# A state-space scan's small products in three bunches a group instead of four, with the last output weights moved ahead of the last norm

## The chip, the core and the metric

One core of a Trainium2 chip runs the whole model in one launch. The metric is device time in microseconds (us): the median of the timed runs. Engines are named as in the profile: PE (matrix products), DVE, ACT and POOL (elementwise work), SP (issues the transfers).

## The reference

One sequence of 512 tokens, width 1024, float32, goes through two layers; each is a mixer and then a channel mixer, both added to the input. The channel mixer (`conv_ffn`) is an up projection to 44 tiles of 128 channels, a causal convolution of three taps, gate times up, and a down projection. Layer 0 mixes by dilated attention. Layer 1 mixes by a scan, and the change is mostly there. Cut to what matters, in chunks of 128 tokens:

```
zxbcdt = h @ w_in                              # z, x, B, C, dt
x, B, C = silu(conv4(x, B, C)); dt = softplus(dt + bias)
a_cs   = cumsum(dt * a) in a chunk;  xdt = x * dt
cb     = C @ B^T                               # one 128x128 block a chunk and group
y_diag = (cb * exp(a_cs_i - a_cs_j), j <= i) @ xdt
states = B^T @ (xdt * exp(a_cs_last - a_cs));  prev = scan of states over the chunks
y      = y_diag + (C @ prev) * exp(a_cs) + d_skip * x
g      = y * silu(z);  y = g * rsqrt(mean(g*g over the group's 256 channels) + eps) * norm_w
out    = x_in + y @ w_out
```

There are 8 groups (B, C and the norm are per group) with 4 heads of 64 channels each, so a group has two x tiles and two z tiles of 128 channels. A last norm follows layer 1.

## The kernel before

Activations lie with 128 channels on the partitions and all 512 tokens along the free dimension. Every projection is done in three float32r products: weights and activations are split into a high and a low part (`hi`/`lo`, `xh`/`xl`, made by ACT and DVE, for z tiles by POOL), and `mm3` multiplies high by high, high by low and low by high. One output tile of 128 channels is thus 24 matmuls of 128x128 by 512 ("a projection"), all of line L127. A weight tile of 512 KB (`raw_...`) is loaded by SP, three in flight, and five pairs `hi`/`lo` exist. Products of projections land in three `mm` banks of PSUM; the small products use three `aux` and two `side` banks.

In layer 1, `project_group(g, ...)` lists six projections of a group: x0, b, c, x1, z0, z1. `scan_group(g, ...)` is a generator that does the rest of a group. Its products, by the names of their outputs:

- px (xs transposed, for each half x = 0 and 1; DVE makes xdt of it and POOL xdd), pb (B transposed, copied to btok), pc (C times B; DVE masks it into cb);
- pst (states, from xdd and btok); a chain of one copy, two multiplications and two additions on DVE turns it into prev;
- py (from lm and xdt) and pf (from C and prev); lm is a row of a_cs copied from HBM to 128 partitions by SP, then four subtractions on DVE, an Exp on ACT and a product with cb on POOL; ee is the Exp of the same rows;
- ss (column sums of gsq, the squares of the gated output yt; DVE makes ms, POOL the power rg) and prg (rg laid along the free dimension), after which yt is scaled and split into `y{g}{x}` high and low.

Output weights are applied group-wise: `w01` (groups 0 and 1), `w23`, `w4`, `w56`, and `w7` in `last_group`, each eight steps (one per 128 output channels); DVE adds each product to the residual xr. A step for one group is 6 matmuls, for two groups 12.

The order on PE within layer 1 is written by hand (`manual_schedule`): `groups` weaves the pieces of `behind(g)`, which are the generator's steps of group g and the norm of group g-1, with a list `fill` of projections of group g+1 and output steps. A group has four bunches of small products with `(17, 24, 21, 38)` as shares of the filling. `last_group` treats group 7, the output steps left over, and the first products of the next channel mixer (`u1_0` to `u1_3`) between the last norm's parts. On DVE, ACT, POOL and mostly SP a scheduler in the compiler orders the work by its own estimates; only a part marked otherwise is fixed.

At the start eight products of ones by ones (`warm`) run while the first weights arrive, and products called v follow. The final channel mixer multiplies gate and up (`au`) and takes its low part (`g21l` for the last pair) on POOL, at L543 and L546.

Of the kernel before, what the change touches and what calls it, by code (L numbers as in the profile page):

```python
# [51 lines left out]
def trunk(ctx: ExitStack, tc: tile.TileContext, A, out):  # L52
# [20 lines left out]
    def side_bank(name):  # L73
        return ps.tile([P, 512], F32, tag="side", name=name, bufs=2)
# [196 lines left out]
    xps = []  # L271
    load, first = v_steps(1, 0, 2)
    warm = side_bank("warm")
    for _ in range(8):
        T.matmul(warm[:, 0:P], ones, ones, start=True, stop=True)
    with tc.manual_schedule(engines={mybir.EngineType.SP}):
        for k in range(KD):
# [250 lines left out]
    def ffn(layer, done):  # L528
        for part, (c0, cn) in enumerate(FF_PARTS):
            gh, gl = [], []  # L530
            for c in range(c0, c0 + cn):
                ab = []
                for gu in range(2):
                    i = 2 * c + gu
                    n = f"u{layer}_{i}"
                    p = project(A["wup"][layer * 44 + i], n)
                    us = t2("us" + n, "us", 3, lp)
                    V.tensor_tensor(us, p, rbc, op=ALU.mult)  # L538
                    a = t2("a" + n, "a", 13, lp)
                    conv(a, us, C_FCW + (layer * 44 + i) * 3, C_FCB + layer * 44 + i, 3)  # L540
                    ab.append(a)
                SC.activation(ab[0], ab[0], AF.Silu)
                G.tensor_tensor(ab[1], ab[0], ab[1], op=ALU.mult)  # L543
                g_h, g_l = high_low(f"g{c}")
                SC.copy(g_h, ab[1])
                G.tensor_tensor(g_l, ab[1], g_h.bitcast(F32), op=ALU.subtract)  # L546
                gh.append(g_h)
                gl.append(g_l)
            n = cn * P

            def load(m):
                i = (layer * len(FF_PARTS) + part) * KD + m
                return (*load_unit(A["wdn"][i][:, :n], f"wd{i}", n), 0)

            def add(m, p):
                V.tensor_tensor(xr[m], xr[m], p, op=ALU.add)  # L556
                if part == len(FF_PARTS) - 1:
                    done(m)
# [106 lines left out]
    def scan_group(g, d, ys):  # L665
# [17 lines left out]
        def states(x):  # L683
            pst = aux_bank("pst")
            for c in range(3):
                cs = slice(c * P, (c + 1) * P)
                T.matmul(pst[:, cs], btok[:, cs], xdd[x][:, cs], start=True, stop=True)
            t = t2("prev", "prev", 1, lp)
            SC.copy(t[:, 0:P], pst[:, 0:P])
            for c in range(1, 3):  # L690
                now, was = slice(c * P, (c + 1) * P), slice((c - 1) * P, c * P)
                V.tensor_tensor(
                    two(t[:, now]), two(t[:, was]),
                    cd3[:, c, heads[x]].unsqueeze(2).to_broadcast([P, 2, 64]), op=ALU.mult,
                )
                V.tensor_tensor(t[:, now], t[:, now], pst[:, now], op=ALU.add)
            prev.append(t)
# [17 lines left out]
                lm.append(t)  # L715
            ee.append(e_)

        def outputs(x):
            py, pf = side_bank("py"), side_bank("pf")


            with tc.manual_schedule(engines={mybir.EngineType.PE}):
                for c in range(NCH):
                    cs = slice(c * P, (c + 1) * P)
                    for hp in (1, 0):
                        T.matmul(
                            py[hp * 64 : (hp + 1) * 64, cs],
                            xdt[x][:, c * P + hp * 64 : c * P + (hp + 1) * 64], lm[2 * x + hp][:, cs],
                            start=True, stop=True,
                        )  # L730
                for c in reversed(range(1, NCH)):
                    T.matmul(  # L732
                        pf[:, c * P : (c + 1) * P], prev[x][:, (c - 1) * P : c * P],
                        ct[:, c * P : (c + 1) * P], start=True, stop=True,
                    )
            yt = t2("yt", "yt", 2, lp)
            V.tensor_tensor(ee[x][:, P:512], ee[x][:, P:512], pf[:, P:512], op=ALU.mult)
            V.scalar_tensor_tensor(
                yt, xs[x], col(C_DSK + 2 * g + x), py, op0=ALU.mult, op1=ALU.add
            )  # L740
            V.tensor_tensor(yt[:, P:512], yt[:, P:512], ee[x][:, P:512], op=ALU.add)
            V.tensor_tensor(yt, yt, d[f"z{x}"], op=ALU.mult)
            sq = t2("gsq", "sq", 2)
            SC.activation(sq, yt, AF.Square)
            return yt, sq
# [5 lines left out]
            T.transpose(pb[:, c * P : (c + 1) * P], bt[:, c * P : (c + 1) * P], ident)  # L751
        btok = t2("btok", "btok", 1, lp)
        SC.copy(btok[:, 0:384], pb[:, 0:384])
        pc = aux_bank("pc")
        for c in range(NCH):
            cs = slice(c * P, (c + 1) * P)
            T.matmul(pc[:, cs], bt[:, cs], ct[:, cs], start=True, stop=True)
# [3 lines left out]
            tri.unsqueeze(1).to_broadcast([P, NCH, P]), op=ALU.mult,  # L761
        )
        yield
        decays(0)
        states(0)
        by_token(1)
        yield
        y0, sq0 = outputs(0)
        decays(1)
        states(1)  # L770
        yield
        y1, sq1 = outputs(1)
        V.tensor_tensor(sq0, sq0, sq1, op=ALU.add)
        yield
        rg = sm.tile([P, 4], F32, tag="rg", name="rg")
# [44 lines left out]
    writes = [[], [], w01[:4], w01[4:], w23[:4], w23[4:], w4[:4]]  # L820
    scans = []

    def behind(g):

        scans.append(scan_group(g, tiles[g], ys))
        for i in range(4):
            next(scans[g])
            if g and i < 2:
                next(scans[g - 1], None)
            yield  # L830

    def groups():
        decays = decay_rates()
        next(decays)
        for i, f in enumerate(ahead[0] + ahead[1][:1]):
            f()
            if i == 1:
                next(decays)
        next(decays, None)
        for g in range(NSG - 1):  # L840
            a, w = ahead[g + 1], writes[g]
            if g == 0:
                fill = a[1:]
            elif g == NSG - 2:
                fill = [a[0], a[1], w[0], w[1], a[2], w[2], w[3], a[3]]
            else:
                fill = a[:3]
                n = -(-len(w) // 3)
                for i, f in enumerate(a[3:]):
                    fill = fill + w[i * n : (i + 1) * n] + [f]  # L850
            weave(behind(g), (17, 24, 21, 38) if g else (1, 1, 1, 2), fill)

    def last_group():

        z0, z1 = ahead[NSG - 1][4:]
        core = behind(NSG - 1)  # L860
        for fill in ([z0, w4[4]], [z1, w4[5]], [w4[6], w4[7], w56[0]], w56[1:5]):
            next(core)
            for f in fill:
                f()
        scan = scans[-1]
        load7, w7 = write_groups([7], ys)
        next(scan)
        w56[5]()
        load7(0)
        units = []  # L870

        def unit(i):
            name = f"u1_{i}"
            units.append((
                load_unit(A["wup"][44 + i], name), side_bank(name) if i in (1, 2) else mm_bank(name), name
            ))

        def part(i, *ks):
            if i == len(units):
                unit(i)  # L880
            (hi, lo), t, _ = units[i]
            for k in ks:
                mm3(t, hi, lo, k, xh[k], xl[k], k == 0, k == KD - 1)

        with tc.manual_schedule(engines={mybir.EngineType.DVE, mybir.EngineType.Activation}):
            next(scan, None)
            w56[6]()
            w56[7]()
            unit(0)
            load7(1)  # L890
        for m in range(5):
            w7[m]()
        part(0, 0)
        w7[5]()
        part(0, 1)
        part(1, 0)
        w7[6]()
        part(0, 2)
        part(1, 1)
        part(2, 0)  # L900
# [12 lines left out]
        part(3, *range(4, KD))  # L913
        for _, t, name in units:
            early[name] = t

    with tc.manual_schedule(engines={mybir.EngineType.PE}):
        groups()
        last_group()


    def finish(load, operand, cn):
# [135 lines left out]
```

## Time and profile before

| what | value |
|---|---|
| median of 3 runs | 1686.44 us (1686.26 to 1686.98) |
| the profiled execution, its own time | 1686.95 us |
| its span, first to last instruction | 1685.2 us |
| PE, DVE, ACT, POOL busy | 98%, 63%, 41%, 27% |
| mean granted clock of PE | 0.995 |
| scan layer, first x0 projection to first product of u1 | 871 to 1310 us: 439.0 us, PE busy 421.85 |

In the profile a row of a timeline gives the start and the length in us, then engine, line, operation, output and inputs; brackets give the engine's idle time before it and what ended that. A row of groups ends with total busy time and mean ns of one, then the idle time before. A float32 product of small tiles leaves two records, a float32r one or a transpose one. PEclk is the granted share of PE's clock, 1.00 or 0.50 here.

### The profile page before, as it was taken

Reading aid. Unit: us, or ns where it says so; the run is one execution under the profiler, and the core shown is the slowest. Engines: PE = TensorE matmul, PEld = TensorE weight load, DVE = VectorE, ACT = ScalarE, POOL = GpSimd, SP = SyncE. Lnnn points to the kernel's source line nnn. Section 1 sums busy time; section 2 is a strip of 40 time slices with the busy share of each in tenths; the row PEclk is TensorE's granted clock in tenths of the full one; section 3 lists DMA queues with packets and bytes.
Section 4 is the critical chain, followed back from the end, with each engine's and each line's share of the span. In section 5 each row is a group of like instructions: output and inputs, shape, how many; then the busy total and the mean of one; then the engine's idle time right before and its main releaser. Section 6 shows DMA issues by size and latency. Waiting matters only on the chain.

```text
span 1685.2 us, 21510 instructions
## 1 busy us (share of the span) xinstructions
PE 1656.1 (98%) x8224; PEld 1403.1 (83%) x8224; DVE 1066.3 (63%) x1794; ACT 698.8 (41%) x1022; POOL 462.8 (27%) x305
## 2 busy tenths in 40 slices
PE   9999999999999999999999899999989999999997
PEld 8888888888888888888888777888878788888887
DVE  5366564366657745745657788777786784574564
ACT  5233332333245423423346665455552542342345
POOL 0443443144413211211242222332230341121124
PEclk9999999999999999999999999999999999999999
DMA  6322222222223223223233232333221332322323
GB/s 225 112 77 74 88 76 88 92 84 75 81 95 125 100 88 113 100 87 102 75 115 119 88 100 94 105 102 100 101 82 42 121 104 86 111 100 88 113 76 125
DMA packets 52342, 165.56 MB, mean 98 GB/s; under 512 B 5840, under 2 KB 8144, under 8 KB 52240
## 3 DMA queue, kind: packets, MB, share of 16 engines
q1 hardware_dynamic: 51152, 163.15, 28.7%
q8 instruction: 65, 1.06, 0.3%
q10 hardware_dynamic: 1088, 1.05, 0.2%
q14 instruction: 37, 0.30, 0.1%
HBM read 162.01 MB, written 2.16 MB: 97 GB/s over the span
## 4 chain that ended last, share of the span: by engine, by line
PE 91%; DVE 5%; issue 1%; ACT 1%; POOL 1%; DMA 1%; POOLq 0%; SPq 0%; DVEq 0%; ACTq 0%
PE u L127 28%; PE qk L127 15%; PE wd L127 12%; PE v L127 8%; PE z L127 5%; PE xs L127 5%; PE wso L127 4%; PE b L127 2%; PE wz L127 2%; PE wo L127 1%; PE c L127 1%; PE pp L410 1%; PE pg L423 1%; PE po L418 1%; PE pf L732 1%
## 5 line engine op out<-in xcount | busy, mean ns | idle before, releaser
L127 PE MATMUL u<-xl,hi_u 128*128 128x512 f32 x704 | 270.3, 384 | 0.8 <-DVE xl L176 0.8
L127 PE MATMUL u<-xh,hi_u 128*128 128x512 f32 x704 | 270.4, 384 | 0.0
L127 PE MATMUL u<-xh,lo_u 128*128 128x512 f32 x704 | 270.0, 384 | 0.0
L543 POOL TENSOR_TENSOR au<-au,au 128x512 f32<-128x512 f32 x44 | 57.9, 1316 | 434.9 <-DVE au L523 414.3
L118 ACT CAST hi_u<-raw_u 128x1024 fp32r<-128x1024 f32 x88 | 91.2, 1044 | 196.9 <-PE u L127 101.9
L523 DVE SCALAR_TENSOR_TENSOR au<-usu,par,au 128x510 f32<-128x510 f32 (+1 forms) x176 | 160.9, 919 | 5.9 <-ACT au L521 1.0
L325 POOL TENSOR_TENSOR rotqk<-rotqk,sr 32x512 f32<-32x512 f32 x48 | 91.8, 1913 | 257.6 <-DVE rotqk L324 214.4
L127 PEld LDWEIGHTS u<-xl,hi_u 128*128 128x128 f32 x704 | 131.9, 187 | 26.8 <-DVE xl L176 1.8
L127 PEld LDWEIGHTS u<-xh,lo_u 128*128 128x128 f32 x704 | 131.9, 187 | 25.3
L127 PEld LDWEIGHTS u<-xh,hi_u 128*128 128x128 f32 x704 | 131.9, 187 | 25.3
L127 PE MATMUL qk<-xh,hi_qk 128*128 128x512 f32 x384 | 149.1, 388 | 0.0
L127 PE MATMUL qk<-xl,hi_qk 128*128 128x512 f32 x384 | 148.2, 386 | 0.0
L127 PE MATMUL qk<-xh,lo_qk 128*128 128x512 f32 x384 | 147.1, 383 | 0.0
L538 DVE TENSOR_TENSOR usu<-u,rbc 128x512 f32<-128x512 f32 x88 | 60.5, 690 | 112.7 <-PE u L127 103.3
L119 DVE TENSOR_TENSOR lo_u<-raw_u,hi_u 128x1024 fp32r<-128x1024 f32 x88 | 112.9, 1289 | 22.1 <-ACT hi_u L118 22.1
L556 DVE TENSOR_TENSOR xr<-xr,wd 128x512 f32<-128x512 f32 x40 | 27.2, 687 | 116.7 <-PE wd L127 116.7
L118 ACT CAST hi_qk<-raw_qk 128x1024 fp32r<-128x1024 f32 x48 | 50.1, 1045 | 102.5 <-PE v L127 52.5
L321 DVE TENSOR_TENSOR qk<-qk,cr 128x512 f32<-128x512 f32 x48 | 33.0, 688 | 91.0 <-PE qk L127 90.7
L118 ACT CAST hi_wd<-raw_wd 128x1024 fp32r<-128x1024 f32 (+1 forms) x56 | 52.4, 951 | 76.7 <-PE wd L127 39.7
L127 PEld LDWEIGHTS qk<-xh,lo_qk 128*128 128x128 f32 x384 | 72.0, 188 | 13.2
L127 PEld LDWEIGHTS qk<-xh,hi_qk 128*128 128x128 f32 x384 | 72.0, 188 | 12.8
L127 PEld LDWEIGHTS qk<-xl,hi_qk 128*128 128x128 f32 x384 | 72.1, 188 | 12.3
(635 smaller groups left out, 3969.4 us busy)
## 6 DMA issues: line engine op xcount, KB each, us to landing
raw_u<-in_wup SPq DMA_DIRECT2D x88, 512.0 KB, 3.2
raw_qk<-in_wqk SPq DMA_DIRECT2D x48, 512.0 KB, 3.2
raw_wd<-in_wdn SPq DMA_DIRECT2D x32, 512.0 KB, 3.2
raw_wd<-in_wdn SPq DMA_DIRECT2D x24, 384.0 KB, 3.1
raw_xs<-in_win SPq DMA_DIRECT2D x16, 512.0 KB, 3.2
raw_z<-in_win SPq DMA_DIRECT2D x16, 512.0 KB, 3.3
lm<-rows SPq DMA_DIRECT2D x32, 256.0 KB, 4.1
raw_wso<-in_wso SPq DMA_DIRECT2D x16, 512.0 KB, 3.2
```

Of the source, the lines that this page charges most:

```text
L118: SC.copy(hi[:, s], raw[:, s])
L119: low.tensor_tensor(lo[:, s], raw[:, s], hi.bitcast(F32)[:, s], op=ALU.subtract)
L127: T.matmul(in_turns(dst), w, in_turns(x), start=first, stop=last)
L321: V.tensor_tensor(at(t), of(p), of(cr), op=ALU.mult)
L325: G.tensor_tensor(rot[R, :], rot[R, :], sr[R, :], op=ALU.mult)
L410: T.transpose(pp[:, b * P : (b + 1) * P], pr[:, b * P : (b + 1) * P], ident)
L418: T.matmul(po[:, ii], v0[h][:, b * P : (b + 1) * P], pts[i][:, (b - i + 1) * P : (b - i + 2) * P], start=b == max(i - 1, 0), stop=b == i,)
L423: T.matmul(pg[:, ii], vt[g, half][i][:, es], pts[i][:, (g + 1) * P : (g + 2) * P], start=g == 1, stop=g == 2,)
L523: V.scalar_tensor_tensor(dst[:, j:], src[:, : S - j], col(c_w + taps - 1 - j), dst[:, j:], op0=ALU.mult, op1=ALU.add,)
L538: V.tensor_tensor(us, p, rbc, op=ALU.mult)
L543: G.tensor_tensor(ab[1], ab[0], ab[1], op=ALU.mult)
L556: V.tensor_tensor(xr[m], xr[m], p, op=ALU.add)
```

## The change

1. `scan_group` is cut into three bunches a group: A is px of half 0, pb, px of half 1 and pc (and ss of the group before); B is both pst (and prg of the group before); C is both py and then both pf. The two halves have their own prev (two buffers instead of one), and py and pf of half 1 use aux banks, pc a side bank.
2. `between(g)` writes out what stands between two bunches: two projections, with output steps added to them. For the last group all eight steps of `w4` stand between A and B, z1 and two steps of `w56` between B and C, and two more of `w56` behind C.
3. `last_rows` puts one step of `w56` between ss and prg of the last group and three behind prg, and loads both units of `w7` and the first of u1 ahead of that.
4. The decay rates' last products (pa, prow) stand ahead of x0 of group 1 instead of behind it.
5. Eleven instead of eight `warm` products. The last pair of the last channel mixer is multiplied and split on DVE instead of POOL.

```diff
-    for _ in range(8):
+    for _ in range(11):
         T.matmul(warm[:, 0:P], ones, ones, start=True, stop=True)
...
-                G.tensor_tensor(ab[1], ab[0], ab[1], op=ALU.mult)
+                by = V if layer == 1 and c == NFF - 1 else G
+                by.tensor_tensor(ab[1], ab[0], ab[1], op=ALU.mult)
...
-                G.tensor_tensor(g_l, ab[1], g_h.bitcast(F32), op=ALU.subtract)
+                by.tensor_tensor(g_l, ab[1], g_h.bitcast(F32), op=ALU.subtract)
...
-            t = t2("prev", "prev", 1, lp)
+            t = t2("prev", "prev", 2, lp)
...
-        def outputs(x):
-            py, pf = side_bank("py"), side_bank("pf")
+        def products(x):
+            py, pf = (side_bank("py"), side_bank("pf")) if x == 0 else (aux_bank("py"), aux_bank("pf"))
...
+            def carried():
                 for c in reversed(range(1, NCH)):
                     T.matmul(
                         pf[:, c * P : (c + 1) * P], prev[x][:, (c - 1) * P : c * P],
                         ct[:, c * P : (c + 1) * P], start=True, stop=True,
                     )
+                return py, pf
+            return carried
+        def outputs(x, py, pf):
...
         SC.copy(btok[:, 0:384], pb[:, 0:384])
-        pc = aux_bank("pc")
+        by_token(1)
+        pc = side_bank("pc")
...
         yield
-        decays(0)
-        states(0)
-        by_token(1)
+        for x in range(2):
+            states(x)
+        for x in range(2):
+            decays(x)
         yield
-        y0, sq0 = outputs(0)
-        decays(1)
-        states(1)
-        yield
-        y1, sq1 = outputs(1)
+        carried = [products(x) for x in range(2)]
+        (y0, sq0), (y1, sq1) = (outputs(x, *banks) for x, banks in enumerate([f() for f in carried]))
         V.tensor_tensor(sq0, sq0, sq1, op=ALU.add)
...
-        for i in range(4):
+        for i in range(3):
             next(scans[g])
...
+    def between(g):
+        if g < NSG - 1:
+            x0, b, c, x1, z0, z1 = ahead[g + 1]
+        if g < NSG - 3:
+            after = ahead[g + 2][0]
+            return [
+                [[b, c], [x1, z0], [z1, after]],
+                [[b, c], [x1, z0], [z1, after]],
+                [[b, c], [x1, z0], [z1, *w01[:2], after]],
+                [[b, w01[2], c], [x1, w01[3], z0], [z1, *w01[4:6], after]],
+                [[b, w01[6], c], [x1, w01[7], z0], [z1, *w23[:2], after]],
+            ][g]
+        if g == NSG - 3:
+            return [b, w23[2], c], [x1, w23[3], z0], [z1, *w23[4:6]]
+        if g == NSG - 2:
+            return [x0, b], [c, x1], [z0, *w23[6:]]
+        return w4, [ahead[g][5], *w56[:2]], w56[2:4]
...
-        for i, f in enumerate(ahead[0] + ahead[1][:1]):
+        for i, f in enumerate(ahead[0]):
...
         next(decays, None)
-        for g in range(NSG - 1):
...
-            weave(behind(g), (17, 24, 21, 38) if g else (1, 1, 1, 2), fill)
+        ahead[1][0]()
+        for g in range(NSG):
+            for _, fill in zip(behind(g), between(g)):
+                for f in fill:
+                    f()
...
         next(scan)
-        w56[5]()
+        w56[4]()
         load7(0)
+        load7(1)
...
+        unit(0)
         with tc.manual_schedule(engines={mybir.EngineType.DVE, mybir.EngineType.Activation}):
             next(scan, None)
-            w56[6]()
-            w56[7]()
-            unit(0)
-            load7(1)
+            for m in range(5, KD):
+                w56[m]()
```

The order on PE, small products of group 1 (and the norm of group 0), the rows of L127 between them left out. Before:

```order
L674 MATMUL px<-ident,axs_7085 128x128 x4
L751 MATMUL pb<-ident,ab_7161 128x128 x3
L757 MATMUL pc<-ac_7238,ab_7161 128x128 x4
L196 MATMUL ss<-ones,gsq 128x1 x4
...
L687 MATMUL pst<-xdd,btok 128x128 x3
L674 MATMUL px<-ident,axs_7329 128x128 x4
L208 MATMUL prg<-ident,rg 128x128 x4
...
L726 MATMUL py<-lm,xdt 64x128 x8
L732 MATMUL pf<-ac_7238,prev 128x128 x3
L687 MATMUL pst<-xdd,btok 128x128 x3
```

A fourth bunch, py and pf of half 1, follows. Now, on the same engine and for the same group:

```order
L676 MATMUL px<-ident,axs_7103 128x128 x4
L760 MATMUL pb<-ident,ab_7173 128x128 x3
L676 MATMUL px<-ident,axs_7309 128x128 x4
L767 MATMUL pc<-ac_7212,ab_7173 128x128 x4
L196 MATMUL ss<-ones,gsq 128x1 x4
...
L689 MATMUL pst<-xdd,btok 128x128 x6
L208 MATMUL prg<-ident,rg 128x128 x4
...
L728 MATMUL py<-lm,xdt 64x128 x16
L736 MATMUL pf<-ac_7212,prev 128x128 x6
```

Both px now stand in the first bunch, both pst in the second, and both halves' py and pf in the third.

The order on POOL from a low part of z of group 2 (lo_z) through group 1's work to the power rg that prg of group 0 needs. Before:

```order
L119 TENSOR_TENSOR lo_z_7745<-raw_z_7743,hi_z_7744 128x1024
L677 TENSOR_TENSOR xdd<-xdt,dec 128x384
L714 TENSOR_TENSOR lm<-lm,cb 128x512 x4
L202 TENSOR_TENSOR rg<-ms,mhalf 128x4
L119 TENSOR_TENSOR lo_z_7779<-raw_z_7777,hi_z_7778 128x1024
```

Now:

```order
L119 TENSOR_TENSOR lo_z_7695<-raw_z_7693,hi_z_7694 128x1024
L119 TENSOR_TENSOR lo_z_7770<-raw_z_7768,hi_z_7769 128x1024
L679 TENSOR_TENSOR xdd<-xdt,dec 128x384 x2
L716 TENSOR_TENSOR lm<-lm,cb 128x512 x4
L202 TENSOR_TENSOR rg<-ms,mhalf 128x4
```

Ahead of rg there now stand a second lo_z and a second xdd.

The order on ACT at the last group, from the Exp of its rows (ee) to the first cast of the weights for w56 (hi_wso). Before:

```order
L706 ACTIVATE ee<-lm 64x384 x2
L647 ACT_TABLE_LOAD
L647 ACTIVATE ab_9775<-ab_9775 128x512
L744 ACTIVATE gsq<-yt 128x512
L713 ACT_TABLE_LOAD
L713 ACTIVATE lm<-lm 128x512 x2
L118 CAST hi_z_10106<-raw_z_10105 128x1024
L521 ACTIVATE ac_9888<-usc_9886,par 128x512
L118 CAST hi_wso_10216<-raw_wso_10215 128x1024
```

Now:

```order
L708 ACTIVATE ee<-lm 64x384 x4
L649 ACT_TABLE_LOAD
L649 ACTIVATE axs_9821<-axs_9821 128x512
L118 CAST hi_z_10120<-raw_z_10119 128x1024
L753 ACTIVATE gsq<-yt 128x512 x2
L715 ACT_TABLE_LOAD
L715 ACTIVATE lm<-lm 128x512 x3
L645 ACT_TABLE_LOAD
L645 ACTIVATE usz_9899<-usz_9899 128x512
L715 ACT_TABLE_LOAD
L715 ACTIVATE lm<-lm 128x512
L118 CAST hi_wso_10154<-raw_wso_10153 128x1024
```

The cast now stands behind all four ee and all four lm of the last group.

The order on DVE at the same place, from xdt of the last group to the first addition of a w4 product. Now:

```order
L678 TENSOR_TENSOR xdt<-px,dtt 128x512
L119 TENSOR_TENSOR lo_wso_10155<-raw_wso_10153,hi_wso_10154 128x1024
L678 TENSOR_TENSOR xdt<-px,dtt 128x512
L119 TENSOR_TENSOR lo_wso_10161<-raw_wso_10159,hi_wso_10160 128x1024
L769 TENSOR_TENSOR cb<-pc,tri 128x512
L201 TENSOR_SCALAR ms<-ss 128x4
L812 TENSOR_TENSOR xr_4036<-xr_4036,wso_9976 128x512
```

Before, the first four w4 products were added ahead of that xdt; now the first addition stands behind two low parts.

More of the change, by code (lines that the diff above doesn't have):

```diff
@@ L716, in decays @@
             ee.append(e_)
-        def outputs(x):
-            py, pf = side_bank("py"), side_bank("pf")
[L722 to L730, printed above, removed]
+        def products(x):
+            py, pf = (side_bank("py"), side_bank("pf")) if x == 0 else (aux_bank("py"), aux_bank("pf"))
+            for c in range(NCH):
+                cs = slice(c * P, (c + 1) * P)
+                for hp in (1, 0):
+                    T.matmul(
+                        py[hp * 64 : (hp + 1) * 64, cs],
+                        xdt[x][:, c * P + hp * 64 : c * P + (hp + 1) * 64], lm[2 * x + hp][:, cs],
+                        start=True, stop=True,
+                    )
+            def carried():
                 for c in reversed(range(1, NCH)):
@@ L819, in trunk @@
     w01, w23, w4, w56 = (write_groups(gs, ys)[1] for gs in ([0, 1], [2, 3], [4], [5, 6]))
-    writes = [[], [], w01[:4], w01[4:], w23[:4], w23[4:], w4[:4]]
     scans = []
@@ L839, in groups, with last_rows @@
         next(decays, None)
-        for g in range(NSG - 1):
[L841 to L850, printed above, removed]
-            weave(behind(g), (17, 24, 21, 38) if g else (1, 1, 1, 2), fill)
[L853 to L864, printed above, removed]
+        ahead[1][0]()
[3 more added lines that the diff above has]
+                    f()
+    def last_rows():
         scan = scans[-1]
@@ L918, in trunk @@
         groups()
-        last_group()
+        last_rows()
     def finish(load, operand, cn):
```

## The prediction

> **What bounds the kernel now.** I read the page's totals and its chain first, then PE's waits, then the stretches.
>
> ```profile
> span 1685.2 us, 21510 instructions
> PE 1656.1 (98%) x8224; PEld 1403.1 (83%) x8224; DVE 1066.3 (63%) x1794; ACT 698.8 (41%) x1022; POOL 462.8 (27%) x305
> PE 91%; DVE 5%; issue 1%; ACT 1%; POOL 1%; DMA 1%; POOLq 0%; SPq 0%; DVEq 0%; ACTq 0%
> ```
>
> PE is the bound: 29 us of the span are not PE, and an edit can save only those, products run at half clock, or overhead between products. So the next view is who keeps PE waiting in the scan layer, 866 to 1340 us (total, times, longest):
>
> ```profile
> PE pf L732 <- DVE prev L696: 8.9, 4, 4.9
> PE prg L208 <- POOL rg L202: 1.7, 2, 1.1
> PE px L674 <- ACT axs L647: 1.7, 1, 1.7
> PE pc L757 <- ACT ac L647: 1.6, 1, 1.6
> PE pb L751 <- ACT cdec L630: 1.4, 1, 1.4
> PE wso L127 <- DVE xr L804: 0.8, 1, 0.8
> PE ss L196 <- DVE gsq L773: 0.7, 1, 0.7
> ```
>
> The places of these waits come from PE's timeline (start, length, then in brackets the idle time before), and the stretches show the clock (time, busy time of PE, PEld, DVE, ACT, POOL, then PEclk):
>
> ```profile
> 921.60 0.83 PE L687 MATMUL pst<-xdd,btok 128*128 128x128 f32 x6
> 934.14 1.65 PE L732 MATMUL pf<-ac,prev 128*128 128x128 f32 x6 [4.88 <-DVE prev L696]
> 971.50 1.16 PE L208 MATMUL prg<-ident,rg 128*128 128x128 f32 x8 [1.09 <-POOL rg L202]
> 1249.33 1.16 PE L757 MATMUL pc<-ac,ab 128*128 128x128 f32 x8 [1.60 <-ACT ac L647]
> ...
> 932.00:938.80 6.80, 4.66 (x17) 4.28 (x18) 6.80 (x14) 4.33 (x7) 0.48 (x1) 0.50 0.39 130
> 1030.00:1240.00 210.00, 210.00 (x1158) 178.02 (x1157) 159.25 (x294) 114.83 (x155) 52.37 (x35) 1.00 0.30 101
> 1256.00:1263.10 7.10, 4.77 (x29) 3.91 (x28) 4.69 (x4) 3.53 (x5) 6.49 (x5) 1.00 0.15 59
> 1263.10:1266.50 3.40, 3.40 (x13) 2.82 (x12) 3.40 (x9) 0.81 (x2) 0.83 (x1) 0.50 0.42 154
> ```
>
> Three things are to be seen. In groups 0 to 2 PE waits 11.4 us: all of pf (8.9), pb (1.4) and the first prg (1.09). From 1030 to 1240, where output products stand between the scan's bunches, it never waits. In the last group it waits another 4.6 us (1.6 + 0.7 + 1.7 + the second prg's 0.6). Twice a wait drags the clock to half: 4.66 busy us in the first such stretch and 3.40 in the second did half the work, which costs 2.3 and 1.7 us more.
>
> **The change, part by part.** *Bunches.* Every group's small products now form three bunches, A (px, pb, px, pc, ss), B (pst, pst, prg) and C (py, py, pf, pf), instead of four; with eight groups eight bunches go. The chain in order of time prices one:
>
> ```profile
> 895.68 10.56 PE z L127 x48
> 1057.93 5.46 PE xs L127 x24
> 1063.40 5.36 PE b L127 x24
> 1096.65 10.72 PE z L127 x48
> ```
>
> Two projections unbroken take 10.56, so one takes 5.28. The pair that ends at a bunch takes 0.16 more, xs that follows a bunch 0.18 more, b, which ends at one, 0.08. I take 0.30 a bunch: 8 x 0.30 = **-2.4** (from -1.3, at 0.08 twice, to -2.7, at 0.34).
>
> *Waits of groups 0 to 2.* pf waits because its pst stands only one projection ahead of it, with a long chain of additions on DVE between. Now both pst stand two projections (10.6) ahead of pf, and prev has two buffers. In group 0 pf came 12.5 after pst began (921.60), with DVE held up between; two projections and both py (10.6 + 2.1) cover just that. pb's 1.4 goes since the decay rates' products move ahead of a projection. So -11.4 and -2.3 of clock.
>
> What is late next is prg of group 0, at B of group 1: its rg stands on POOL behind all of that group's work.
>
> ```profile
> L714 POOL TENSOR_TENSOR lm<-lm,cb 128x512 f32<-128x512 f32 x32 | 43.4, 1375 | 13.5 <-ACT lm L713 7.6 <-DVE ms L201 3.7 <-DVE cb L759 2.0
> L119 POOL TENSOR_TENSOR lo_z<-raw_z,hi_z 128x1024 fp32r<-128x1024 f32 x16 | 40.0, 2497 | 111.3 <-ACT hi_z L118 111.3
> L677 POOL TENSOR_TENSOR xdd<-xdt,dec 128x384 f32<-128x384 f32 x16 | 19.1, 1192 | 158.1 <-DVE xdt L676 156.8 <-ACT btok L753 1.3
> L202 POOL TENSOR_TENSOR rg<-ms,mhalf 128x4 f32<-128x4 f32 x8 | 8.5, 1063 | 28.0 <-DVE ms L201 28.0
> ```
>
> POOL does two lo_z, two xdd, four lm and rg: 5.0 + 2.4 + 5.5 + 1.1 = 14.0, and can begin only when ACT has cast hi_z, behind the squares of group 0's outputs; those end about when A starts (ss, in A, needs them). With 3 for the casts that is 17 to 18 us after A begins. PE comes to prg after A (2.7: by prg's row four products take about 1, transposes half), two projections (10.6) and six pst (1.3): 14.6. Wait: 3. With the wait for ss, put at the 0.7 of its row above, and a half-clock stretch of 1.7 behind it (the smaller of the two seen), that is 5.4; I take +5.5. Bounds: 1.8 (prg's 1.09, ss 0.7) and 9 (a wait like the longest, 4.9, its 2.3, and 1.8 elsewhere). Net of the first groups **-8.2**.
>
> *The last group.* Its waits, 4.6 and 1.7 of clock, go with the old order. The new one puts all eight w4 products between A and B, where they need mm banks that DVE's xr additions free, six matmuls of 0.22 each. On DVE the first of these now stands behind lo of the next weights, and that waits for ACT, where both casts stand behind four ee, four lm, two squares, two Silu and four table loads:
>
> ```profile
> L706 ACT ACTIVATE ee<-lm 64x384 f32<-64x384 f32 x32 | 16.7, 523 | 12.5 <-DVE yt L741 12.0
> L647 ACT ACT_TABLE_LOAD x14 | 18.0, 1283 | 10.5 <-DVE axs L523 7.8 <-DVE ab L523 2.6
> L713 ACT ACTIVATE lm<-lm 128x512 f32<-128x512 f32 x32 | 19.0, 623 | 5.7 <-DVE lm L709 5.5
> L118 ACT CAST hi_wso<-raw_wso 128x1024 fp32r<-128x1024 f32 x16 | 16.6, 1038 | 6.5 <-PE z L127 3.6 <-issue 1.3 <-PE b L127 1.0
> 938.12 0.55 DVE L741 TENSOR_TENSOR yt<-yt,ee 128x384 f32<-128x384 f32 x1
> L119 DVE TENSOR_TENSOR lo_wso<-raw_wso,hi_wso 128x1024 fp32r<-128x1024 f32 x16 | 19.5, 1221 | 9.3 <-ACT hi_wso L118 9.3
> L804 DVE TENSOR_TENSOR xr<-xr,wso 128x512 f32<-128x512 f32 x40 | 27.1, 681 | 11.8 <-PE wso L127 11.8
> ```
>
> ACT's first ee waits for DVE's yt of the group before: in group 0 that addition ended 2.9 us after pf (935.79 to 938.67), and both halves now come at once, so 4. Then 4 x 0.52 + 4 x 1.28 + 8 x 0.62 (squares and Silu like lm) + two casts at 1.04 = 14.3 to the end of hi_wso; then on DVE two lo (2.4) and xdt, cb and xr (0.68 each): 4.4. Sum 22.7 after C of group 6. PE wants the fourth w4 bank after 48 long products (10.6, and 0.3 for the bunch), A (2.7) and three w4 (4.0): 17.6. Wait 5.1, and such a length cost 2.3 of clock once: +7.4 against -6.3, net **+1.1** (bounds -6.3, the wait gone, and +6, a wait twice as long).
>
> *End of the layer.* The last w56 rows and the loads of w7 and u1 move ahead of the last norm, so three w56 products (36 matmuls, 8 us) cover what two covered: the 0.8 for xr: **-0.8** (0 to -0.8).
>
> *End of the channel mixer.* g21's product and low part go from POOL to DVE:
>
> ```profile
> 1643.96 0.60 PE L127 MATMUL wz<-g21h,hi_wd 128*128 128x256 f32 x3 [0.16 <-ACT g21h L545]
> 1645.31 0.38 PE L127 MATMUL wz<-g21l,hi_wd 128*128 128x256 f32 x1 [0.74 <-POOL g21l L546]
> ```
>
> At most 0.9 is there; two DVE rows of 0.68 replace two of POOL at 1.3: **-0.8** (0 to -0.9).
>
> *Three more warm-up products*, six records:
>
> ```profile
> 1.05 3.78 PE L275 MATMUL warm<-ones 128*128 128x128 f32 x16 [1.05 <-DVE mhalf L100]
> 5.50 2.05 PE L127 MATMUL v<-hi_v,xh 128*128 128x512 f32 x4 [0.67 <-DVE hi_v L116]
> 9.06 1.70 PE L127 MATMUL v<-lo_v,xh 128*128 128x512 f32 x4
> 10.60 1.04 PE L127 MATMUL v<-hi_v,xh 128*128 128x512 f32 x4
> ```
>
> The first 12 products of v take 5.1 us (0.43 each, later 0.22): half clock until 10.5. Six records more take 1.3 and fill the 0.67 of idle time, so v starts about 0.4 late. If the clock then comes one stretch of 3.4 (as at 1263.10) sooner, at 7.1, three products go slow and nine fast: done at 9.1, 1.5 sooner. I take **-1.2**, since xl and lo come from DVE when they came before (bounds +0.5, clock unchanged, and -2.3, all twelve fast). The Trainium skill, "TensorE: Matmul & The Clock Gate", Part 1, says that the gate watches a free-running window of about 3.4 us, so that the moment of release shifts from run to run; by that the term would stand anywhere between these bounds.
>
> *At nothing:* ACT's table loads fall from 42 to 24, ACT being 41% busy; the rows' copies go out three, a weight load, one: 4 us each to land against a group's 50, so cover would have to shrink tenfold.
>
> Sum: -2.4 - 8.2 + 1.1 - 0.8 - 0.8 - 1.2 = **-12.3** on the profiled execution's 1686.95, so 1674.6. The median of the runs lies 0.5 below that execution: **1674.1 us**.
>
> **Rivals.** *Fewer stalls:* the 5.5, the 7.4 or both don't come, because squares and casts run earlier than I put them: 1668.6, 1666.7 or 1661.2. For it: PE waits nowhere between 1030 and 1240. Against: both chains are sums of rows that exceed their cover.
> *Larger stalls:* the bounds of both (+3.5, +4.9) and prg of group 2 too (+3): from 1677.6, one of them, to 1685.5, all. For it: rg of group 2 also stands behind four lm.
> *Slower:* POOL becomes late in every group. py of both halves now needs all four lm at C; if POOL's 14 us a group, begun 3 into A, pass the 26 from A to C (2.7, 10.6, B's 2, 10.6), each of eight groups waits, say, the 2.3 that the last group idles in 7.1, and pays 1.7: 32, so 1706. It decides once POOL's 14 grow by 9; POOL's 52.37 busy us of 210 in 1030 to 1240 speak against.
> *The gate forgives short waits:* PE's idle time behind ss and prg falls into two pieces with products between them. If only one unbroken gap of 3.4 us halved the clock, the 1.7 would not be paid: 1672.4. Against: 1263.10 followed two gaps of 1.7 and 0.6. The Trainium skill's rule in "TensorE: Matmul & The Clock Gate" (HAM oscillation) is this one, no idle gap above some 3.4 us; the trace does not agree, with 2.3 us of idle time in 7.1.
> *No effect:* the order of PE's products is changed by hand, so only if gains and stalls cancel.
>
> **Numbers.** 0.2% (3.4 us) is about what a measurement tells from no change: faster is below 1683.1, slower above 1689.8. Forecast 0.55, gate 0.05, fewer stalls 0.20, larger 0.15 (a third of it within 0.2%), slower 0.03, none 0.02. Faster 0.90, same 0.07, slower 0.03. Range 1666 to 1681: it leaves out half of fewer stalls, half of larger ones and the last two.
>
> **What would show it.** Right: pf without a wait in groups 0 to 2; one wait at prg near 970 and one at the fourth w4 product, each with half clock; v fast from about 7 us; groups 3 to 6 shorter by 0.3 each. Wrong: a wait in every group at B or C, PE held for weights behind the rows' copies, or w4 without a stall.

## The result and the profile after

The changed kernel took 1677.76 us (median of 4 runs, 1676.15 to 1679.52) against 1686.35 (1685.33 to 1686.98): a ratio of 0.995, 95% interval 0.9933 to 0.9967. It is faster by 8.6 us; 12.3 were forecast. The execution in the profile took 1678.73 us, its span 1676.9, 8.3 less than that of before.

The head of the page after, and then who keeps PE waiting from 866 to 1340 us (total, times, longest):

```profile
span 1676.9 us, 21508 instructions
PE 1653.3 (99%) x8230; PEld 1405.4 (84%) x8230; DVE 1073.8 (64%) x1796; ACT 671.9 (40%) x1004; POOL 468.6 (28%) x303
```

```profile
PE prg L208 <- POOL rg L202: 6.7, 2, 4.4
PE wso L127 <- DVE xr L812: 4.9, 1, 4.9
PE ss L196 <- DVE gsq L781: 0.3, 1, 0.3
```

pf, px, pc and pb wait no longer. PE's timeline shows where the waits left are (idle time in brackets), and the stretches behind them show the clock (length, then busy time of PE, PEld, DVE, ACT and POOL, then PEclk, the share of DMA and GB/s):

```profile
939.64 1.60 PE L736 MATMUL pf<-ac,prev 128*128 128x128 f32 x12
972.03 2.08 PE L208 MATMUL prg<-ident,rg 128*128 128x128 f32 x8 [4.40 <-POOL rg L202]
1018.40 1.41 PE L208 MATMUL prg<-ident,rg 128*128 128x128 f32 x8 [2.31 <-POOL rg L202]
1254.13 0.79 PE L127 MATMUL wso<-y40h,hi_wso 128*128 128x512 f32 x1 [4.91 <-DVE xr L812]
```

```profile
972.00:979.00 7.00, 6.97 (x22) 5.90 (x23) 5.91 (x13) 3.82 (x7) 0.00 (x0) 0.56 0.22 75
1018.00:1025.40 7.40, 7.00 (x28) 5.94 (x29) 6.31 (x14) 3.83 (x7) 0.34 (x1) 0.77 0.20 71
1254.10:1258.20 4.10, 4.07 (x10) 3.21 (x11) 2.28 (x4) 1.05 (x1) 4.10 (x4) 0.51 0.43 136
```

pf waits nowhere. prg waits in groups 1 and 2, and the fourth w4 product waits 4.91. Behind each of the three the clock falls to half: the means of 0.56, 0.77 and 0.51 take in some time at full clock.

The span by landmarks of PE's timeline (a stage runs from the first product named to the next):

| stage | before, us | after, us | difference | forecast |
|---|---|---|---|---|
| start to the scan's first x0 | 871.29 | 870.96 | -0.3 | -1.2 |
| to px of group 0 | 41.59 | 41.75 | +0.2 | 0 |
| groups 0 to 2 (to px of group 3) | 142.45 | 138.36 | -4.1 | -9.1 |
| groups 3 and 4 | 103.77 | 103.30 | -0.5 | -0.6 |
| groups 5 to 7, to ss of the last norm | 171.99 | 169.79 | -2.2 | -0.6 |
| to the first wz | 307.36 | 307.31 | 0 | 0 |
| wz and the end | 46.75 | 45.43 | -1.3 | -0.8 |

Of the 12.3 forecast, 4.0 are missing in all. Groups 0 to 2 alone fall short by 5.0, and that is at prg; the start falls short by 0.9, and the last groups and the end give 2.1 more than forecast. POOL's timeline of group 1 shows the queue that prg waits for, ACT's what stands ahead of the second cast there, and DVE's the queue in front of the additions at w4 (with ACT's cast in the first row's bracket):

```profile
954.43 2.38 POOL L119 TENSOR_TENSOR lo_z<-raw_z,hi_z 128x1024 fp32r<-128x1024 f32 x1 [26.24 <-ACT hi_z L118]
958.88 2.37 POOL L119 TENSOR_TENSOR lo_z<-raw_z,hi_z 128x1024 fp32r<-128x1024 f32 x1 [2.08 <-ACT hi_z L118]
961.22 2.54 POOL L679 TENSOR_TENSOR xdd<-xdt,dec 128x384 f32<-128x384 f32 x2
963.72 6.85 POOL L716 TENSOR_TENSOR lm<-lm,cb 128x512 f32<-128x512 f32 x4
970.52 1.45 POOL L202 TENSOR_TENSOR rg<-ms,mhalf 128x4 f32<-128x4 f32 x1
```

```profile
954.26 1.67 ACT L715 ACTIVATE lm<-lm 128x512 f32<-128x512 f32 x3
955.95 1.28 ACT L645 ACT_TABLE_LOAD   x1
957.24 0.63 ACT L645 ACTIVATE usz<-usz 128x512 f32<-128x512 f32 x1
957.78 1.03 ACT L118 CAST hi_z<-raw_z 128x1024 fp32r<-128x1024 f32 x1
```

```profile
1249.86 1.23 DVE L119 TENSOR_TENSOR lo_wso<-raw_wso,hi_wso 128x1024 fp32r<-128x1024 f32 x1 [4.68 <-ACT hi_wso L118]
1253.41 1.87 DVE L812 TENSOR_TENSOR xr<-xr,wso 128x512 f32<-128x512 f32 x3
```

### The profile page after: what moved, and what is told of

Read it like the earlier page. It is cut to its first block, busy times and chain, and to the rows that moved or that the text cites. A ratio compares the mean times of both kernels' runs of the same rounds, so it can differ in the third digit from the quotient of the medians.

```text
span 1676.9 us, 21508 instructions
## 1 busy us (share of the span) xinstructions
PE 1653.3 (99%) x8230; PEld 1405.4 (84%) x8230; DVE 1073.8 (64%) x1796; ACT 671.9 (40%) x1004; POOL 468.6 (28%) x303
## 3 DMA queue, kind: packets, MB, share of 16 engines
q8 instruction: 65, 1.06, 0.3%
## 4 chain that ended last, share of the span: by engine, by line
PE 89%; DVE 4%; issue 2%; POOL 2%; ACT 1%; DMA 1%; SPq 0%; POOLq 0%; ACTq 0%; DVEq 0%
PE u L127 28%; PE qk L127 15%; PE wd L127 12%; PE v L127 6%; PE wso L127 5%; PE z L127 4%; PE xs L127 4%; PE wz L127 2%; PE b L127 2%; PE wo L127 2%; PE c L127 1%; PE pp L410 1%; PE pg L423 1%; POOL lm L716 1%; PE po L418 1%
## 5 line engine op out<-in xcount | busy, mean ns | idle before, releaser
L127 PE MATMUL u<-xh,hi_u 128*128 128x512 f32 x704 | 270.3, 384 | 0.0
L127 PE MATMUL u<-xl,hi_u 128*128 128x512 f32 x704 | 270.1, 384 | 0.2 <-DVE xl L176 0.2
L127 PE MATMUL u<-xh,lo_u 128*128 128x512 f32 x704 | 270.0, 383 | 0.0
L127 PEld LDWEIGHTS u<-xl,hi_u 128*128 128x128 f32 x704 | 131.9, 187 | 25.8 <-DVE xl L176 0.6
L127 PEld LDWEIGHTS u<-xh,lo_u 128*128 128x128 f32 x704 | 131.9, 187 | 25.3
L127 PEld LDWEIGHTS u<-xh,hi_u 128*128 128x128 f32 x704 | 131.9, 187 | 25.1
L127 PE MATMUL qk<-xh,hi_qk 128*128 128x512 f32 x384 | 149.1, 388 | 0.0
L127 PE MATMUL qk<-xl,hi_qk 128*128 128x512 f32 x384 | 148.2, 386 | 0.0
L127 PE MATMUL qk<-xh,lo_qk 128*128 128x512 f32 x384 | 147.1, 383 | 0.0
L127 PEld LDWEIGHTS qk<-xh,lo_qk 128*128 128x128 f32 x384 | 72.0, 188 | 13.3
L127 PEld LDWEIGHTS qk<-xh,hi_qk 128*128 128x128 f32 x384 | 72.0, 188 | 12.8
L127 PEld LDWEIGHTS qk<-xl,hi_qk 128*128 128x128 f32 x384 | 72.1, 188 | 12.4
```

Source lines behind the costliest of these rows:

```text
L127: T.matmul(in_turns(dst), w, in_turns(x), start=first, stop=last)
```

## Experiments

Each kernel was timed on the same chip as the kernel before, which gave medians of 1686.35 to 1687.07. The runs of one kernel spread over 3 us and more, so small terms have to be read in the traces, at their own place.

**z_dve: POOL's queue in front of prg.**

```diff
-        p = project(A["win"][i], name, V if c_conv is not None else G)
+        p = project(A["win"][i], name, V if c_conv is not None or i in (16, 17, 22, 23) else G)
```

> The changed kernel with one edit: the low parts of z of groups 2 and 3 (two each) are made by DVE instead of POOL, so that the power rg of groups 0 and 1 stands behind two xdd and two lm instead of two lo_z, two xdd and four lm. Theory (POOL's queue makes prg late): in the changed kernel rg of group 0 began at 970.52 behind lo_z 4.75, a gap of 2.08 for the second cast, xdd 2.54 and lm 6.85; without lo_z and with two lm less it begins by 967, PE wants prg at 967.6, so both prg waits (4.4 and 2.3) fall below 0.5 and the two half-clock stretches behind them (2.1 and 1.4) go: 1677.8 - 10 = 1668, 1667 to 1670. Rival (DVE is what is late: ms was ready only at 963.1, and DVE now has 1.22 more for each lo_z): the waits stay at 2 or more, or move to pst or px, and the time stays within 3 of 1677.8.

Measured: 1671.3 us, ratio 0.9903 (0.9888 to 0.9918). POOL's rows and PE's prg in group 1, and all of PE's waits from 866 to 1340:

```profile
964.12 3.42 POOL L716 TENSOR_TENSOR lm<-lm,cb 128x512 f32<-128x512 f32 x2
967.50 1.02 POOL L202 TENSOR_TENSOR rg<-ms,mhalf 128x4 f32<-128x4 f32 x1
969.49 1.06 PE L208 MATMUL prg<-ident,rg 128*128 128x128 f32 x8
```

```profile
PE wso L127 <- DVE xr L812: 4.9, 1, 4.9
PE ss L196 <- DVE gsq L781: 1.1, 1, 1.1
PE xs L127 <- DVE usz L643: 0.6, 1, 0.6
```

rg ends at 968.5, and prg follows pst without a wait, in group 2 as well. Groups 0 to 2 take 128.47 instead of 138.36, 9.9 less, as expected. DVE is not what is late, but it now makes PE wait 0.8 more at ss and 0.6 at xs. So the 9.9 are a net value: the two prg waits with all that hangs on them cost about 11.3. The time itself fell less than expected (1667 to 1670): the profiled execution is 8.4 shorter, since the start took 0.8 more, the stretch to px of group 0 another 0.5 and groups 5 to 7 0.3.

**fill: idle time and clock apart.**

```diff
+        for _ in range(idle):
+            T.matmul(p[:, 0:P], ones, ones, start=True, stop=True)
...
-        prg = along_free(rg, "prg", side_bank)
+        prg = along_free(rg, "prg", side_bank, {0: 18, 1: 9}.get(g, 0))
```

> The changed kernel with products of ones by ones put ahead of prg, into the bank that prg then overwrites: 18 in group 1 and 9 in group 2 (4.0 and 2.0 us at full clock by the 0.11 of a record in warm at full clock). POOL's rg is not touched. Theory (the two waits are paid twice, once as idle time and once as half clock behind it): rg ends when it did, the idle time falls to about 0.5 in each group, the xs projections behind prg take 5.5 instead of 7.56 and 6.87, and the time falls by 3.5: 1674.3, 1673 to 1676. Rival (the slow products behind prg have another cause, the products of f32 or DVE's load at that place): the xs projections stay at 7 us, and the time stays at 1677.8, or rises by what the filling overshoots, under 1.

Measured: 1675.86 us, ratio 0.9933 (0.9918 to 0.9948). The filling and prg on PE, and the stretches behind prg in groups 1 and 2:

```profile
968.40 4.18 PE L208 MATMUL prg<-ones 128*128 128x128 f32 x36
973.00 1.16 PE L210 MATMUL prg<-ident,rg 128*128 128x128 f32 x8 [0.41 <-POOL rg L202]
```

```profile
974.00:979.00 5.00, 5.00 (x25) 4.16 (x24) 4.45 (x11) 1.70 (x5) 0.00 (x0) 1.00 0.30 105
1017.00:1022.00 5.00, 5.00 (x24) 4.21 (x23) 5.00 (x13) 1.66 (x5) 0.00 (x0) 1.00 0.32 105
```

With PE kept busy by products that compute nothing, the clock stays at 1.00, and the two xs projections behind prg take 5.49 and 5.43 instead of 7.56 and 6.87: 3.5 less, as expected. Groups 0 to 2 are 4.9 shorter. Of the other 1.4, prg itself at full clock gives 1.1 (the first product behind it comes 0.82 and 0.24 sooner after prg's start); that the rest is a stop which the filling replaces is not shown. So of the 11.3 some 4.6 are clock and 6.7 idle time. The rival, that the products behind prg are slow by themselves, falls.

**w4_split, z_hi_dve, zs_hi_dve: the additions in front of w4.** PE's order, and then who makes the casts:

```diff
-        return w4, [ahead[g][5], *w56[:2]], w56[2:4]
+        return [ahead[g][5], *w4[:4]], [*w4[4:], *w56[:2]], w56[2:4]
```

```diff
-                SC.copy(hi[:, s], raw[:, s])
+                (high.tensor_copy if high is not None else SC.copy)(hi[:, s], raw[:, s])
...
-                units[i] = [load_unit(A["wso"][2 * g + i], f"wso{g}{i}") for g in gs]
+                units[i] = [load_unit(A["wso"][2 * g + i], f"wso{g}{i}", high=V if gs == [5, 6] and i == 0 else None) for g in gs]
```

> The changed kernel with one edit in PE's order of the last group: projection z1 and four w4 steps stand between bunches A and B, and four w4 steps and two w56 steps between B and C, instead of all eight w4 steps between A and B. Theory (the fourth w4 product waits for a bank whose addition on DVE stands behind lo of the next weights, which waits for ACT's cast at 1248.8): the first w4 bank is now wanted back 5.3 us later, and the Silu and table load for z1 leave ACT's queue ahead of the cast; the wait of 4.9 falls below 1.2 and the half clock behind it (1.9) goes: 1677.8 - 6.3 = 1671.5, 1670.5 to 1673.5. Rival (DVE only holds the banks until its cast comes, whatever PE does, so that z1's bank becomes the one that is late): a wait of 3 to 5 at the third w4 product, and 1677 to 1679.

> The kernel z_dve with one more edit: the high parts of the first two weights of w56 are cast by DVE itself instead of ACT. PE's order is that of the changed kernel. Theory (in the last group DVE stood idle for 4.68 us at lo of these weights because ACT's cast came behind lm, Silu and table loads, and the additions that free w4's banks stood behind it): that idle time goes, at 0.9 for each cast of 1024 on DVE; the first addition comes some 3 us sooner, the wait at the fourth w4 product falls from 4.9 to between 1.5 and 3, the half clock behind it (2.4) shrinks or goes: 1671.3 - 3.5 = 1668, 1666.5 to 1670. Rival (DVE's own work ahead of the addition is what takes the time, since the casts are added to it): a wait of 4 or more, and 1671.

> z_dve, w4_split and the two casts on DVE together. Theory: the prg waits are gone as in z_dve (1671.3), the first bank is wanted back 5.3 us later than in the changed kernel and is freed some 3 us sooner, so no wait above 0.7 is left in the last group, against 4.9 and 2.4 of half clock: 1671.3 - 6.5 = 1664.8, 1663.5 to 1667. Rival (something else holds PE in the last group once DVE is on time, such as POOL's xdd for pst, or z1's weights): one wait of 2 or more at another product, and 1668 to 1671.

w4_split took 1677.12 us, ratio 0.9934 (0.9917 to 0.995). PE's waits from 1200 to 1300 in its trace:

```profile
PE wso L127 <- DVE usz L643: 2.0, 1, 2.0
PE wso L127 <- DVE xr L812: 1.4, 2, 0.8
PE ss L196 <- DVE gsq L781: 0.2, 1, 0.2
```

From px of group 7 to the last ss it takes 79.65 against 82.53, 2.9 less instead of 6.3, and half clock is gone there. The time hardly fell: it was expected at 1670.5 to 1673.5. Its runs spread from 1674.63 to 1679.08, and the profiled one is the slowest: 1.6 of half clock followed the wait at its first norm (rb, 2.14), which the edit does not touch. Both theories are half right. DVE's lo still stood idle for 5.16 us, as the rival said, because the Silu ahead of ACT's cast is that of z0 and not, as I had assumed, of z1; and PE's wait of 2.0 is at the third w4 product, the rival's place, but shorter than its 3 to 5.

z_hi_dve took 1666.04 us, ratio 0.9879 (0.9864 to 0.9893), zs_hi_dve 1663.69 us, ratio 0.9866 (0.9852 to 0.9881). PE's waits, 866 to 1340, of the one and then of the other:

```profile
PE xs L127 <- DVE usz L643: 2.2, 1, 2.2
PE wso L127 <- DVE xr L812: 1.3, 1, 1.3
PE ss L196 <- DVE gsq L781: 0.3, 1, 0.3
```

```profile
PE xs L127 <- DVE usz L643: 1.5, 1, 1.5
PE wso L127 <- DVE xr L812: 0.6, 1, 0.6
PE ss L196 <- DVE gsq L781: 0.6, 2, 0.3
```

With PE's order left alone, the two casts on DVE bring the wait at w4 from 4.93 to 1.34 with no half clock behind it, and the stage from 82.90 (z_dve) to 76.92. That ACT's cast held DVE, and DVE the banks, is thereby shown. z_hi_dve is 0.5 faster than the range expected (1666.5 to 1670), zs_hi_dve lies inside its own. The split takes another 0.2 off that stage and half of the wait that is left. zs_hi_dve is the fastest version: 23 us under the kernel before, 14 under the changed one. What remains in the z_dve kernels is a wait at xs (x0 of group 4), for DVE's usz. In the changed kernel the same usz ended at 1045.55, only 0.2 ahead of xs, so little makes it late; in z_hi_dve, where the wait is longest, DVE had stood idle 0.49 and 0.70 for the rows' copies. That the low parts which DVE took over are the cause is not shown.

**ends and ms_act: the start and the end.**

```diff
-    for _ in range(11):
+    for _ in range(8):
...
-                by = V if layer == 1 and c == NFF - 1 else G
+                by = G
```

> The changed kernel with its two smallest edits undone: eight warm products instead of eleven, and the last pair of the last channel mixer multiplied and split on POOL again. Both are read in the trace at their own places. Theory at the start (PE's earlier start is taken back at the first norm, whose ms stands on DVE behind a low part of v that waits for a weight transfer): the first norm's ss begins near 27.7 instead of 25.2, but rb begins at 30.1 as before, and the start costs 0.1 or less. Rival, the step of the prediction: the start costs 1.2. At the end: wz's first 173 products take 1.3 longer again (21.80 against 20.48). Sum by the theory +1.4: 1679.2; by the rival +2.6: 1680.4. The traces decide, since these are near what timing can tell.

Measured: 1680.86 us, ratio 0.9957 (0.9942 to 0.9971). PE's rows at the start of ends, with eight warm products, and in the changed kernel with eleven:

```profile
1.05 3.78 PE L275 MATMUL warm<-ones 128*128 128x128 f32 x16 [1.05 <-DVE mhalf L100]
25.85 0.95 PE L196 MATMUL ss<-ones,ssum 128*128 128x1 f32 x8
30.12 1.16 PE L208 MATMUL rb<-ident,rcol 128*128 128x128 f32 x8 [1.83 <-POOL rcol L202]
```

```profile
25.23 0.95 PE L196 MATMUL ss<-ones,ssum 128*128 128x1 f32 x8
30.07 1.16 PE L208 MATMUL rb<-ident,rcol 128*128 128x128 f32 x8 [1.74 <-POOL rcol L202]
```

In the kernel before, ss began at 27.76 and rb at 30.12. rb comes at the same time whether PE arrives early or late. And ss is early in ends too (25.85, where 27.7 was expected), with eight warm products: there v's products follow each other at 0.22 to 0.25 from 5.9 us on, in the profiled execution of before, also with eight, only from 10.5. So v was slow in that one execution, and not because of the number of warm products. What holds rb is DVE's queue, in the changed kernel:

```profile
27.55 1.23 DVE L119 TENSOR_TENSOR lo_v<-raw_v,hi_v 128x1024 fp32r<-128x1024 f32 x1 [1.46 <-ACT hi_v L118]
28.70 0.15 DVE L201 TENSOR_SCALAR ms<-ss 128x4 f32<-128x4 f32 x1
```

ms is ready to be made at 26.2 and is made at 28.7. At the end, wz's products up to the first ss take 21.78 in ends, 21.80 before, 20.48 after: the edit on g21 is worth 1.3. The time of ends is nearer to the rival's 1680.4 than to the theory's 1679.2, but its runs go from 1677.56 to 1681.36, and in its trace the scan's first x0 begins only 0.5 later than in the changed kernel (871.46 and 870.96), which is less than the other kernels with eleven differ among themselves (870.78 to 873.28).

In ms_act ACT makes ms of the first norm (Copy with scale and bias) in place of DVE.

> The changed kernel with one edit at the start: ms of the first norm is made by ACT instead of DVE, where it stood behind a low part of v whose weight arrives late. Theory (that place on DVE's queue takes back what faster products won): ACT makes ms right behind its last cast of v, near 27.7, the power near 28.9, rb begins at about 28.9 instead of 30.1, and all of it lasts to the first norm of layer 0's channel mixer (521.67 in the changed kernel, 520.5 here): the time falls by 1.2, to 1676.6. Rival (the start is bound by the transfers of the weights as a whole): PE waits for the next weights instead, that norm begins at 521.5 or later, and the time stays at 1677.8.

Measured: 1676.91 us, ratio 0.9946 (0.993 to 0.9963). The power on POOL and rb on PE:

```profile
27.80 1.98 POOL L205 TENSOR_TENSOR rcol<-ms,mhalf 128x4 f32<-128x4 f32 x1 [27.36 <-ACT ms L202]
29.84 1.16 PE L211 MATMUL rb<-ident,rcol 128*128 128x128 f32 x8 [1.15 <-POOL rcol L205]
```

ms came where it was expected, but the power took 1.98 instead of 1.02, and rb came 0.2 sooner, not 1.2. The norm of the channel mixer began at 521.42 instead of 521.67. The power now runs beside DVE's lo_v (27.69 to 28.92) and not behind it; whether that is why it took longer stays open. That the time met the 1676.6 expected is luck: groups 0 to 2 took 134.75 instead of 138.36, because prg of group 2 waited 1.35 without half clock and half clock behind prg of group 1 was shorter.

**undo_pa and prev1: what removed the old waits.**

```diff
-        next(decays, None)
         ahead[1][0]()
+        next(decays, None)
```

```diff
-            t = t2("prev", "prev", 2, lp)
+            t = t2("prev", "prev", 1, lp)
```

> The changed kernel with one edit undone: the decay rates' last products (pa, prow) stand behind x0 of group 1 again, right ahead of bunch A of group 0. Theory (pb takes pa's bank, which ACT's Exp to cdec still reads, as in the kernel before): the wait of 1.4 at pb comes back, in the trace between px and pb of group 0, and perhaps as much for the second px, whose bank held prow; no half clock behind it, since waits below 1.6 were not followed by any: +1.4 to +3, 1679.2 to 1680.8. Rival (the new bunch hides it): no wait above 0.3 there, 1677.8. The trace decides.

> The changed kernel with one buffer for prev instead of two, all else as it is: the second half's chain of copy, two multiplications and two additions can begin only when pf of the first half has read prev, and pf of the second half stands right behind. Theory (the second buffer is what let both chains run ahead of pf, and removed the 11.4 of waits in groups 0 to 2 and kept the others free of them): pf waits 3 to 5 in each of the eight groups, and half clock follows in most: +24 to +55, 1702 to 1733. Rival (two projections between the bunches are what mattered, the chain of the second half is short once pst is done): 1 or less in each group and no half clock, +8 or less, up to 1686.

undo_pa took 1680.33 us, ratio 0.9962 (0.9947 to 0.9977); prev1 1737.76 us, ratio 1.03 (1.0274 to 1.0326). The one row of undo_pa, and the only wait of prev1 in the layer:

```profile
915.74 0.55 PE L760 MATMUL pb<-ident,ab 128*128 128x128 f32 x3 [1.40 <-ACT cdec L632]
```

```profile
PE pf L736 <- DVE prev L698: 59.6, 8, 10.8
```

pb's 1.40 comes back to the digit. With one buffer, pf of the second half waits 2.6 to 10.8 in every group, and there is half clock at each of the eight. In seven of them that is more than the 3 to 5 expected, and the time lies above the 1702 to 1733 given. The second buffer of prev is what the three bunches stand on.

## Why the prediction was right and where it was not

**Right.** pf's waits went (prev1 shows by what), as did pb's (undo_pa). prg of group 0 became late in POOL's queue. The wait at the fourth w4 product was put at 5.1 with 2.3 of clock, and was 4.91 with 2.0; the additions were due 22.7 after the end of C of group 6, and the first ended some 23 after it. Groups 3 and 4 gain 0.24 each; 0.30 a bunch was forecast.

**The step that failed is the +5.5 for prg.** About 11.3 came in its place, of which z_dve brought back 9.9 net. Its parts: the wait in group 1 was 4.40 instead of 3. POOL began at A + 2.6 (3 in the forecast), but its 14.0 us of work took 17.5: it stood idle for 2.08 ahead of the second lo_z, since ACT had three lm Exp, a table load and a Silu ahead of the second cast; an lm took 1.71 and rg 1.45, where the groups' means of before gave 1.375 and 1.06. So rg ended 20.1 after A began; PE was there at 15.8, where 14.6 was forecast. The means of a view over eight groups were low for the group that mattered. Then prg of group 2 waited 2.31 as well. The same queue stood there (two lo_z, two xdd, four lm, rg); I had seen it, and left it to the rival "larger stalls" at +3, instead of running the sum for A of group 2. And the clock was paid behind both waits, 2.1 and 1.4 on xs and 1.1 on prg itself, not once at 1.7. So the larger-stalls rival came in half: for prg, not for w4. The measured 1677.8 is its smallest value (1677.6) and not the 1674.1 of the sum, and the range held because it took in half of that rival.

**The warm-up step (-1.2) failed too**, at the clause that lost time would stay won: ms of the first norm stands on DVE behind a late low part of v, and that chain, which I did not follow, sets rb at 29.6 to 30.3 in every trace. v was fast from 5.7, as the forecast's sign asked, but with eight products (ends) it was so from 5.9 too. The eleven products bring nothing that the traces show.

**Too small were the ends**: -2.2 for groups 5 to 7 where -0.6 was forecast, and -1.3 at g21 where at most 0.9 seemed to be there. I priced a stop by the idle time in its bracket. Two long products on either side of a stop of 0.33 us (before, at 1023) start 0.71 apart instead of 0.22, and the next comes 0.11 late: 0.27 more than the bracket. Before, groups 5 to 7 and the layer's end had six stops, now two; groups 0 to 2 had seven, now three; g21 had two. At some 0.2 to 0.27 a stop, an estimate from that one stop, this gives about 1, 1 and 0.5, which would be most of what the sums lacked. No run tests it.

**The gate rival falls**: an idle time of 2.31 was enough to cost 1.4 us of half clock on xs, and fill, which took only the idle time away, got it back. So does "slower": POOL is late in two groups and no other. Faster was right, and the range held.

## What to carry to other kernels

When products are pulled together into fewer bunches, what was needed in between is late next: follow each of the small results that the next bunch needs through the queue of its engine, for every group whose surroundings differ, with the durations of that place and not the mean. An in-order engine that waits for another's cast holds all that stands behind it; giving the waiting engine the cast itself was worth more here than rearranging the products. Time won ahead of a chain that does not move is only waited away at that chain.

## What the runs showed of the hardware

- Whether half clock follows a wait of medium length is not told by its length. Over the ten traces without prev1, each of the twelve waits of 4.4 us or more in the scan layer was followed by it (0.7 to 2.5 us lost on the long products behind). Of fourteen single waits between 1.7 and 2.4, prev1's first norm among them, five were (1.3 to 1.7 lost); none alone below 1.6 was. The wait at rb cost 1.6 of clock at 2.14 and nothing at 1.74 or 2.10.
- What tells it is where the wait lies on a grid. In each of the eleven traces all changes of the granted clock lie whole multiples of 3.413 us apart (within 0.002), and the grid lies differently in each. PE's idle time within one step of 3.413 decides: of the steps at full clock up to 1640 us, all 24 with 1.86 us or more of it were followed by half clock, none with 1.79 or less was, and of four between, two were. So prg of group 2 met half clock behind a wait of 1.82 that lay within one step (w4_split, first two rows: 1.82 idle, then PEclk 0.50) and none behind one of 1.93 that an edge cut into 1.48 and 0.45 (undo_pa, last two):

```profile
1018.14:1021.55 3.41, 1.59 (x14) 1.40 (x13) 2.72 (x3) 1.16 (x2) 2.23 (x2) 1.00 0.16 65
1021.55:1024.96 3.41, 3.41 (x10) 2.62 (x9) 2.97 (x6) 1.44 (x4) 0.00 (x0) 0.50 0.19 50
```

```profile
1014.91:1018.32 3.41, 1.93 (x15) 1.67 (x13) 3.34 (x3) 0.00 (x0) 3.41 (x3) 1.00 0.44 154
1018.32:1021.73 3.41, 2.96 (x17) 2.69 (x18) 2.32 (x5) 2.60 (x5) 0.40 (x1) 1.00 0.00 0
```

- Where the grid lies was chance here, and that can be one source of the spread of 3 us among the runs of the changed kernel. The Trainium skill, "TensorE: Matmul & The Clock Gate", Part 1, has a free-running window of 3413 ns, and the grid in these traces agrees. Its rule under "HAM oscillation", no idle gap above about 3.4 us, does not keep one safe here, as the 1.82 above shows.
- The pace of float32r products has two values: 0.2200 us apart in some stretches (the z pair of 10.56 us quoted in the prediction) and 0.2233 in most (the pair of 10.72), with the clock column at 1.00 in both. My price of a bunch compared a pair of the one kind with single projections of the other; 0.20 to 0.27 a group is what the steady groups show.
